# Two mixers of a macaron trunk: work order and delays laid out anew, a merge in six steps, an output norm that keeps the norm of q inside it

## The chip, the cores and the metric

The kernel runs on one core of a Trainium2 chip as one program. The metric is device time in microseconds (us) of one execution. Its engines are named as the profile names them: PE (TensorE matmuls; PEld are its weight loads), DVE (VectorE), ACT (ScalarE), POOL (GpSimd) and SP (SyncE, whose queue issues the transfers). Tensors live in SBUF; PE writes to PSUM, which has eight banks.

## The reference, cut to what matters

256 tokens of width 1024 go through two layers. Each layer is an FFN half step, a mixer and a second FFN half step, all with a norm before and a norm after. The mixer runs a gated DeltaNet (eight heads of 128) and a causal convolution module side by side:

```python
for i in range(DEPTH):
    f = swiglu_ffn(rmsnorm(x, ffn1_norm_pre[i]), ffn1_w_in[i], ffn1_w_out[i])
    x = x + 0.5 * rmsnorm(f, ffn1_norm_post[i])
    h = rmsnorm(x, mix_norm_pre[i])
    qkv, z, beta_logit, a_logit, glu_in, gates = jnp.split(h @ mix_w_in[i], SPLITS, axis=-1)
    y_a = gated_deltanet(qkv, z, beta_logit, a_logit, ...)   # short convolution, l2norm(q), l2norm(k),
                                                             # triangular solve, scan, rmsnorm(o) * silu(z), @ w_o
    y_b = conformer_conv(glu_in, ...)                        # glu, 31-tap convolution, layernorm, silu, @ w_o
    g_a, g_b = jnp.split(jax.nn.sigmoid(gates), 2, axis=-1)
    x = x + rmsnorm((g_a * y_a + g_b * y_b) @ mix_w_out[i], mix_norm_post[i])
    f = swiglu_ffn(rmsnorm(x, ffn2_norm_pre[i]), ffn2_w_in[i], ffn2_w_out[i])
    x = x + 0.5 * rmsnorm(f, ffn2_norm_post[i])
```

The output norm sees o, which is linear in q, and q was divided by its own norm: `o = rmsnorm(o, norm_w) * silu(z)`.

## The kernel before, in words

**Products.** Every large product is made in three matmuls of a split operand (high times high, high times low, low times high). A weight piece of 128 by 1024 comes in by DMA (raw), ACT rounds it (whi), and DVE or POOL makes the rest (wlo). Eight pieces stand in a ring.

**PE's order is written out.** PE runs in program order. The mixer (line 1128) works through the chunks of PLAN (line 38): glu (g0 to g3), keys (k1, ka, kb), values (v0, v1), queries (q0, q1), z0, z1 and the gates a0 to b1. The by-channel chunks (all g, k, v and q but the first two and ka) leave their products in two PSUM banks each, of four; a chunk two later takes the same banks. Then come three output products: the convolution's, the heads', and the common one (proj_out, line 908).

**Small work is slipped in by ticks.** Between the big matmuls of a chunk, after every three matmuls of 512 columns or six of 256, `Lanes.tick` (line 235) is called. When a chunk ends, the jobs that stand beside it in PLAN are added. A job is a generator; each of its steps issues instructions for several engines. DELAY (line 45) gives the ticks before its first step and between steps, AFTER the jobs that must be done before, LATE the ticks between their end and its start. BEFORE names jobs that are run to their end when a chunk's results are taken out (line 1576): vt0 and qt0 by z0 and a0, qt1 by z1 and a1, merge by b0 and b1. In front of the convolution's output product the job cn is run to its end, in front of the heads' product everything is.

**Fillers.** The taps of the long convolution (c0 to c3, conv31, line 1179; `cacc` in the profile) and the triangular solve on POOL (inv, line 1379) have no delays between steps. A tick issues them as long as the engine's estimated time is less than `ahead` (DVE) or `aheadp` (POOL) in front of PE's. The estimate adds up vector_us (line 95) or pool_us for each operation; DVE and POOL keep the program's order there (`in_order`).

**The jobs that the prediction speaks of.** f_... is the take-out of a chunk: for keys, values and queries the short convolution (conv4, line 1203; `c` in the profile), in steps start on ACT, taps on DVE, silu on ACT, for each of two pairs of heads. vt, qt and kt turn values, queries and keys to tokens and take their norms; qt also makes q times k (qk). sim makes the matrices of the triangular solve, inv solves their 32 by 32 diagonal blocks, and merge (line 1407) joins the blocks to 128 by 128 for both groups of four heads: turn the diagonal blocks, multiply below the diagonal (two steps for 64, two for 128), each time with ACT copies from PSUM back to the operands. In the kernel before, most of its steps hold one group or half of one. s0 and s1 (lines 1523, 1541) are the two parts of the scan; s1's first step ends in eight DVE corrections of vr that its second step's product reads. on0 and on (o_scale, line 1710) are the output norm of the two halves of the tokens: squares on ACT, a power on POOL, eight products on DVE. cn and cn1 are the layer norm of the convolution. pre0 and pre1 (line 693) bring the normed x into the next product's layout.

**Line numbers.** The profile's lines are those of helpers: L134 issues for DVE and POOL, L154 is any matmul, L160 a transpose on PE, L189 any ACT operation. Tiles tell the work apart: `mm` is a big product, `tr` a transpose, `gd` a small product.

Of the kernel before, what the change touches and what calls it, by code (L numbers as in the profile page):

```python
# [15 lines left out]
P = 128  # L16
# [30 lines left out]
    "ffn": (3, 2, 8, 12, 0), "pre0": (12, 12, 10, 0, 21, 2), "pre1": (14, 43, 4, 12, 8), "yt0": (10, 0, 10, 10, 26),  # L47
    "yt1": (10, 2, 0, 3, 3), "f_g0": (3, 0, 2, 9, 1), "f_g1": (5, 1, 1, 1), "c0": (0, 16, 0),
    "f_k1": (0, 1, 3, 1, 1, 3), "f_ka": (3, 0, 3), "decays": (12, 4, 2, 15, 4), "dts": (50, 3, 0, 0, 19, 19),
# [15 lines left out]
    "qs": ("qt0", "qt1"), "s0": ("merge", "vt0", "vt1", "qt0", "qt1"), "s1": ("s0",),  # L65
    "cn": ("c0", "c1", "c2", "c3", "s1"), "cn1": ("cn",), "on": ("s1", "on0"), "on0": ("s0", "qs"),
# [6 lines left out]
LATE = {"inv": 20, "cn": 12, "sim0": 5, "sim1": 6, "merge": 7, "dts": 14}  # L73

POOL = {*range(7, 10), *range(11, 14), 16, *range(18, 21), 22, 23, 25, *range(29, 33), 35, 36, 38, 39, *range(41, 45), *range(47, 50), 51, 53, 55, 58, 60, 61, 63, *range(65, 69), *range(70, 73), 77, 78, 85}
# [11 lines left out]
CFG = dict(stat=1000, conv=50, ev=300, tok=4, st=4, post=-800, pre=1000, fin=None, turn=100, tokens=-100, glu=100, dec=200, dts=500, kt=300, vt=0, qt=50, inv=1000, sim=100, merge=-400, scan=50, norm=-800, onorm=-100, yt=-400, w=50, forms=100, far=14, depth=9, land=1.8, slack=1.2, apart=3, beat=1.0, tails=4, ahead=1.5, lag=6, free=3, aheadp=3, lag2=3, bias=2, held=1)  # L87

KIND = {"f_g0": "glu", "f_g1": "glu", "f_g2": "glu", "f_g3": "glu", "decays": "dec", "dts": "dts", "kt0": "kt", "kt1": "kt",
        "vt0": "vt", "vt1": "vt", "qt0": "qt", "qt1": "qt", "qs": "qt", "inv": "inv", "sim0": "sim", "sim1": "sim",  # L90
# [4 lines left out]
def vector_us(name, size, k):  # L95
    return 0.1 + size / 960.0


def pool_us(name, size, k):
    if k.get("op") == ALU.pow:  # L100
        return 0.4 + 0.16 * size
    if name == "tensor_tensor":
        return 0.05 + 2.3e-3 * size if size > 600 else 0.19 + 1.7e-3 * size
    return 0.2 + (4e-3 if name == "tensor_scalar" else 1e-3) * size

# [222 lines left out]
class Stream:  # L328
# [83 lines left out]
    def plan(self, lanes):  # L412
        if lanes is not None:
            self.planned, self.lanes, lanes.stream, self.begun = True, lanes, self, self.pe.at
# [7 lines left out]
        else:  # L422
            for p in self.pieces[self.taken:self.nload]:
                self.force(p)
            self.planned, self.lanes.stream, self.lanes = False, None, None

# [60 lines left out]
    def issue(self, eng, t, p, kind):  # L487
# [4 lines left out]
        for c in p.parts if p.form else [slice(0, n)]:  # L492
            if kind == "sum":
                a, b = (r.part(c) for r in p.ins)
                with prio(self.tc, "w"):
                    eng.tensor_tensor(p.raw.part(c), a, b, op=ALU.subtract)
            elif kind == "high":
                self.to_high(p, c)
            else:
                self.to_low(p, c, eng)  # L500
        setattr(p, {"sum": "summed"}.get(kind, kind), eng.at)
# [38 lines left out]
def trunk(ctx: ExitStack, tc: tile.TileContext, x_in, wfirst, consts, feat, pch, tokp,  # L540
# [587 lines left out]
    def mixer(xt, l, after_mix):  # L1128
# [96 lines left out]
        rq = small(16, "rq", bufs=1)  # L1225
        rq2 = small(16, "rq2", bufs=1)
# [180 lines left out]
        def merge():  # L1407
            ps = [None, None]
            for gp in (1, 0):
                at = AT[gp]  # L1410
                for tb in range(2):
                    ts = slice(tb * 4, tb * 4 + 4)
                    pt = ps_gd()
                    for hl in range(4):
                        for b in (0, 64, 32):
                            bs = slice(b, b + 32)
                            T.matmul(pt[bs, hl, bs], U[gp][bs, tb * 4 + hl, bs], ident[bs, bs], start=True, stop=True)
                    for b in (0, 64, 32):
                        S.copy(at[b:b + 32, ts, b:b + 32], pt[b:b + 32, :, b:b + 32])
                    yield  # L1420
            for gp in (1, 0):
                at, ps[gp] = AT[gp], ps_gd([P, 16, 32])
                for th in range(8):
                    for b in (0, 64):
                        T.matmul(ps[gp][b + 32:b + 64, th, :], at[b:b + 32, th, b + 32:b + 64], at[b:b + 32, th, b:b + 32],
                                 start=True, stop=True)
                for b in (0, 64):
                    S.copy(at[b + 32:b + 64, :, b:b + 32], ps[gp][b + 32:b + 64, 0:8, :])
                W.memset(at[0:32, :, 32:64], 0.0)
                yield  # L1430
            for gp in (1, 0):
                at, u, p = AT[gp], U[gp], ps[gp]
                for th in range(8):
                    for b in (0, 64):
                        T.matmul(p[b:b + 32, 8 + th, :], at[b + 32:b + 64, th, b:b + 32], u[b + 32:b + 64, th, b + 32:b + 64],
                                 start=True, stop=True)
                    T.matmul(p[32:64, 8 + th, :], u[32:64, th, 32:64], at[32:64, th, 0:32], start=True, stop=True)
                for b in (0, 64):
                    S.activation(u[b:b + 32, :, b + 32:b + 64], p[b:b + 32, 8:16, :], AF.Copy, scale=-1.0)
                S.activation(at[32:64, :, 0:32], p[32:64, 8:16, :], AF.Copy, scale=-1.0)  # L1440
                yield

            def inner(gp, th):
                T.matmul(ps[gp][64:128, th, :], AT[gp][0:64, th, 64:128], AT[gp][0:64, th, 0:64], start=True, stop=True)

            def outer(gp, th):
                T.matmul(ps[gp][0:64, th, :], AT[gp][64:128, th, 0:64], U[gp][64:128, th, 64:128], start=True, stop=True)

            ps[1] = ps_gd([P, 8, 64])
            for th in range(8):  # L1450
                inner(1, th)
# [451 lines left out]
```

## Time and profile before

| | |
|---|---|
| median of 3 runs | 1338.12 us (1337.29 to 1340.12) |
| the profiled execution | 1336.74 us, its span 1335.0 us |
| PE, PEld, DVE, ACT, POOL busy | 98%, 83%, 77%, 58%, 28% |
| granted TensorE clock | 0.999 |
| PE's longest waits in total, span | ACT cf 3.4, ACT vT 2.9, ACT qT 2.8 us |
| chain that ended last | PE 66%, DVE 19%, DMA 6%, ACT 5% |

In a row of a timeline stand start, duration, engine, line, operation, result and operands, form and count; in brackets the idle time of the engine before it and what ended that. In a row of the windows stand the stretch and its length, then for PE, PEld, DVE, ACT and POOL the busy time and the number of instructions, the granted clock, the share of the DMA engines and GB/s. In a group of instructions stand its count, its busy time in total, the mean of one in ns, and the idle time before it. In a row of the waits stand who waited for whom, the sum, the number and the longest. A matmul's shown duration is longer than the distance to the next one, since they are pipelined; that distance is what it costs PE. The first mixer lies at about 176 to 482 us, the second at 837 to 1143 us; between and around them are the FFNs.

### The profile page before, as it was taken

The page shows a single profiled execution, that of the slowest core. Times are in us where ns is not written, and L with a number is a line of the kernel's source. Part 1 is how long each engine was busy: PE and PEld are TensorE (multiplying, and loading weights), DVE is VectorE, ACT ScalarE, POOL GpSimd, SP SyncE. Part 2 cuts the span into 40 slices and gives each one's busy share as a digit, 9 for nine tenths or more (in the row PEclk, how much of TensorE's full clock was granted, in tenths as well). Part 3 has the DMA queues.
Part 4 walks back from the last instruction along what each step waited for, and adds up shares of the span by engine and source line. Part 5 has one row for each costly group of instructions (what it writes and reads, how often), then busy time and mean ns, then how long its engine had stood idle before and what let it go on. Part 6 is the DMA issues. An engine that isn't in the chain of part 4 may idle for free.

```text
span 1335.0 us, 20602 instructions
## 1 busy us (share of the span) xinstructions
PE 1310.3 (98%) x7371; PEld 1112.0 (83%) x7371; DVE 1032.8 (77%) x1816; ACT 771.1 (58%) x1259; POOL 369.1 (28%) x332
## 2 busy tenths in 40 slices
PE   9999999999999999999999999999999999999998
PEld 6888879997787888888888888899977878888886
DVE  6889655999975776897577985579999666678973
ACT  7556547675656545565455564577656564555651
POOL 0000017798853200000000000277997431000000
PEclk9999999999999999999999999999999999999999
DMA  8885846562643766857668767464546437487481
GB/s 292 298 282 154 299 158 206 175 210 98 196 154 126 241 222 220 267 175 265 200 226 269 239 199 259 147 235 174 167 133 198 152 134 252 171 275 247 146 286 60
DMA packets 115014, 273.78 MB, mean 205 GB/s; under 512 B 24128, under 2 KB 47712, under 8 KB 114912
## 3 DMA queue, kind: packets, MB, share of 16 engines
q1 hardware_dynamic: 114624, 272.40, 61.2%
q8 instruction: 58, 0.95, 0.3%
q14 instruction: 44, 0.36, 0.1%
q10 hardware_dynamic: 288, 0.07, 0.0%
HBM read 256.68 MB, written 15.75 MB: 204 GB/s over the span
## 4 chain that ended last, share of the span: by engine, by line
PE 66%; DVE 19%; DMA 6%; ACT 5%; issue 3%; POOL 1%; SPq 0%; DVEq 0%; POOLq 0%; ACTq 0%
PE mm L154 61%; DVE wlo L134 6%; DVE cacc L134 4%; PE gd L154 3%; DMA raw<-w2i 2%; DVE c L134 2%; DMA raw<-mw 2%; ACT whi L189 2%; PE tr L160 2%; DVE sum L134 1%; DVE ag L134 1%; DMA x<-x 1%; DVE at L134 1%; DMA raw<-w1i 1%; ACT dt L189 1%
## 5 line engine op out<-in xcount | busy, mean ns | idle before, releaser
L154 PE MATMUL mm<-whi,xt 128*128 128x512 f32 (+1 forms) x1888 | 598.8, 391 | 3.4 <-ACT qT L189 2.2
L189 ACT CAST whi<-raw 128x1024 fp32r<-128x1024 f32 (+1 forms) x424 | 434.6, 1035 | 282.5 <-PE mm L154 63.3
L134 DVE TENSOR_TENSOR wlo<-raw,whi 128x1024 fp32r<-128x1024 f32 (+1 forms) x316 | 375.7, 1211 | 108.8 <-ACT whi L189 106.3
L154 PEld LDWEIGHTS mm<-whi,xt 128*128 128x128 f32 x1888 | 352.8, 188 | 76.7 <-ACT qT L189 3.0
L154 PE MATMUL mm<-wlo,xt 128*128 128x512 f32 (+1 forms) x944 | 364.9, 387 | 0.0
L134 POOL TENSOR_TENSOR wlo<-raw,whi 128x1024 fp32r<-128x1024 f32 (+1 forms) x108 | 253.7, 2366 | 144.7 <-ACT whi L189 142.3
L154 PE MATMUL mm<-whi,act 128*128 128x512 f32 x704 | 218.3, 390 | 0.0
L154 PEld LDWEIGHTS mm<-wlo,xt 128*128 128x128 f32 x944 | 177.7, 188 | 33.1
L134 POOL TENSOR_TENSOR rpost<-ss,exp 128x1 f32<-128x1 f32 x12 | 6.5, 538 | 660.6 <-DVE ss L134 660.6
L134 DVE SCALAR_TENSOR_TENSOR cacc<-hT,pc,cacc 128x254 f32<-128x254 f32 (+28 forms) x464 | 179.3, 463 | 0.2
L154 PE MATMUL mm<-xt,whi 128*128 128x256 f32 x960 | 175.5, 285 | 0.8 <-ACT qT L189 0.6
L154 PEld LDWEIGHTS mm<-whi,act 128*128 128x128 f32 x704 | 132.2, 188 | 27.5
L154 PEld LDWEIGHTS mm<-xt,whi 128*128 128x128 f32 x960 | 149.3, 192 | 1.9 <-ACT qT L189 0.9
L154 PE MATMUL mm<-wlo,act 128*128 128x512 f32 x352 | 137.3, 390 | 1.0 <-DVE wlo L134 1.0
L154 PE MATMUL mm<-xt,wlo 128*128 128x256 f32 x480 | 135.8, 283 | 0.0
L154 PEld LDWEIGHTS mm<-xt,wlo 128*128 128x128 f32 x480 | 91.9, 192 | 0.0
L154 PEld LDWEIGHTS mm<-wlo,act 128*128 128x128 f32 x352 | 66.1, 188 | 15.6 <-DVE wlo L134 2.2
L189 ACT ACTIVATE ag<-mm,rstd 128x256 f32<-128x256 f32 x76 | 33.8, 471 | 31.6 <-PE mm L154 31.5
L189 ACT ACTIVATE jk<-mm 128x512 f32<-128x512 f32 x24 | 14.3, 597 | 64.5 <-PE mm L154 64.5
L134 DVE TENSOR_TENSOR act<-way,act 128x512 fp32r<-128x512 f32 x44 | 30.2, 686 | 21.9 <-ACT act L189 21.9
L134 DVE SCALAR_TENSOR_TENSOR c<-mm,pc,c 128x255 f32<-128x255 f32 (+2 forms) x108 | 43.6, 472 | 2.4 <-ACT c L189 2.4
L134 DVE SCALAR_TENSOR_TENSOR ag<-mm,rstd,ag 128x256 f32<-128x256 f32 x76 | 33.9, 477 | 13.5 <-ACT ag L189 13.5
(215 smaller groups left out, 1458.5 us busy)
## 6 DMA issues: line engine op xcount, KB each, us to landing
raw<-mw SPq DMA_DIRECT2D x168, 512.0 KB, 3.6
raw<-w2i SPq DMA_DIRECT2D x80, 512.0 KB, 5.1
raw<-w1i SPq DMA_DIRECT2D x76, 512.0 KB, 4.9
raw<-w1o SPq DMA_DIRECT2D x44, 512.0 KB, 4.8
raw<-w2o SPq DMA_DIRECT2D x44, 512.0 KB, 4.8
way<-way SPq DMA_DIRECT2D x112, 64.0 KB, 2.1
way<-way SPq DMA_DIRECT2D x28, 256.0 KB, 3.7
wbc<-feat SPq DMA_DIRECT2D x13, 512.0 KB, 4.8
```

Source lines behind the costliest of these rows:

```text
L134: r = op(out, *a, **k)
L154: r = self.eng.matmul(o, w, x, **k)
L160: r = self.eng.transpose(*a)
L189: r = op(out, *a, **k)
```

## The change

The order of the chunks stays but for v1, which comes before g2. Jobs stand beside other chunks: kt1 with k1, kt0 last in kb's list, c3, vt1 and both qt with q0, c2 and s1 with q1, cn1 with z1, on0 with a0. Nearly all delays of the mixer's jobs are new, as are LATE and the set POOL (which weight pieces outside the planned stretch get their low half on POOL). The operation estimate for DVE is larger for all but the smallest operations; the FFNs' plan keeps the old one. The merge runs both groups in one step, one stage apart. The job qs is gone: o is no longer divided by q's norm. Instead q's sum of squares, scaled by RMS_EPS, is added to the mean square of o in the place of the constant RMS_EPS, which gives the same result.

```diff
 PLAN = [
...
+    ("g0", ["f"]),
+    ("k1", ["f", "sim1", "kt1"]),
+    ("ka", ["f", "decays", "dts"]),
+    ("g1", ["f", "c0"]),
+    ("kb", ["f", "sim0", "inv", "c1", "kt0"]),
+    ("g3", ["f"]),
+    ("v1", ["f"]),
+    ("g2", ["f"]),
+    ("q0", ["f", "qt1", "qt0", "c3", "vt1"]),
+    ("q1", ["f", "cn", "s1", "c2"]),
+    ("v0", ["f", "vt0"]),
+    ("z0", ["s0"]),
+    ("z1", ["merge", "cn1"]),
+    ("a0", ["on0"]),
+    ("b0", []),
+    ("b1", []),
+    ("a1", ["on"]),
 ]
```

The delays that the prediction uses:

```diff
-"pre1": (14, 43, 4, 12, 8),            "f_q1": (1, 1, 3, 1, 0, 0, 2),        "f_v0": (1, 0, 1, 1, 0, 0, 0)
+"pre1": (13, 44, 6, 32, 6),            "f_q1": (0, 0, 0, 4, 2, 0, 16),       "f_v0": (0, 0, 1, 4, 0, 25, 10)
-"merge": (4, 3, 2, 2, 2, 3, 2, 2),     "s1": (11, 5, 3, 6, 1, 1),            "cn": (52, 20, 4, 30, 3, 0, 41, 8)
+"merge": (4, 4, 2, 15, 5, 13, 9, 4),   "s1": (18, 0, 0, 15, 0, 10),          "cn": (49, 24, 0, 36, 14, 6, 2, 4)
-"c2": (6, 0, 0, 0), "c3": (19, 20, 24, 44), "dts": (50, 3, 0, 0, 19, 19),    "inv": (76, 4, 9, 0, 14, 16, 9, 1)
+"c2": (20, 20, 10, 6), "c3": (23, 1, 17, 7), "dts": (0, 3, 0, 0, 29, 0),     "inv": (76, 3, 19, 5, 13, 0, 0, 0)
-LATE = {"inv": 20, "cn": 12, "sim0": 5, "sim1": 6, "merge": 7, "dts": 14}
+LATE = {"inv": 18, "cn": 5, "sim0": 7, "sim1": 0, "merge": 8, "dts": 13, "qt0": 0, "s1": 0, "s0": 4, "qt1": 6, "vt0": 2, "vt1": 17, "kt0": 0, "kt1": 2}
-CFG = dict(..., ahead=1.5, ..., aheadp=3, ..., bias=2, ...)
+CFG = dict(..., ahead=1.2, ..., aheadp=2.5, ..., bias=1.5, ...)
 def vector_us(name, size, k):
-    return 0.1 + size / 960.0
+    return (0.126 if size > 40 else 0.07) + size / 960.0
```

The merge's stages are generators of single products, named turned, first, second, third and fourth; each has its ACT copies (turned_out and so on). Turned, first and second use 32-row blocks, third and fourth 64-row blocks. This loop runs them:

```diff
+            stages = [(turned, turned_out), (first, first_out), (second, second_out), (third, third_out), (fourth, fourth_out)]
+            for i in range(len(stages) + 1):
+                if i:
+                    yield
+                at = [(stages[k], gp) for k, gp in ((i, 1), (i - 1, 0)) if 0 <= k < len(stages)]
+                sums = [list(stage[0](gp)) for stage, gp in at]
+                n = 8
+                for th in range(n):
+                    for s in sums:
+                        for go in s[th * len(s) // n:(th + 1) * len(s) // n]:
+                            go()
+                for stage, gp in at:
+                    stage[1](gp)
```

The output norm:

```diff
-            V.tensor_scalar(vq[:, gp * 8:gp * 8 + 8], ss, float(P), P * 1e-6, op0=ALU.mult, op1=ALU.add)
+            V.tensor_scalar(vq[:, gp * 8:gp * 8 + 8], ss, P * RMS_EPS, P * 1e-6 * RMS_EPS, op0=ALU.mult, op1=ALU.add)
...
-        def q_scale():
-            yield from ()
-            power(rq, vq, -0.5)
-            W.tensor_tensor(rq2, rq, rq, op=ALU.mult)
...
-            W.tensor_tensor(ve, rq2t, sso, op=ALU.mult)
-            W.tensor_scalar(v8, v8, 1.0 / P, RMS_EPS, op0=ALU.mult, op1=ALU.add)
+            V.scalar_tensor_tensor(ve, sso, 1.0 / P, vqt, op0=ALU.mult, op1=ALU.add)
             power(r8, v8, -0.5)
-            W.tensor_tensor(ro, ro, rqt, op=ALU.mult)
```

More of the change, by code (lines that the diff above doesn't have):

```diff
@@ L64 @@
     "qt0": ("f_q0", "vt0"), "qt1": ("f_q1", "vt1"),
-    "qs": ("qt0", "qt1"), "s0": ("merge", "vt0", "vt1", "qt0", "qt1"), "s1": ("s0",),
-    "cn": ("c0", "c1", "c2", "c3", "s1"), "cn1": ("cn",), "on": ("s1", "on0"), "on0": ("s0", "qs"),
+    "s0": ("merge", "vt0", "vt1", "qt0", "qt1"), "s1": ("s0",),
+    "cn": ("c0", "c1", "c2", "c3", "s1"), "cn1": ("cn",), "on": ("s1", "on0"), "on0": ("s0", "qt0", "qt1"),
 }
@@ L85 @@
 USERS = {"12": (("t1", "summed"),), "22": (("22", "low"), ("t2", "summed")), "11": (("t3", "low"),), "21": (("21", "low"), ("t4", "summed"))}
-CFG = dict(stat=1000, conv=50, ev=300, tok=4, st=4, post=-800, pre=1000, fin=None, turn=100, tokens=-100, glu=100, dec=200, dts=500, kt=300, vt=0, qt=50, inv=1000, sim=100, merge=-400, scan=50, norm=-800, onorm=-100, yt=-400, w=50, forms=100, far=14, depth=9, land=1.8, slack=1.2, apart=3, beat=1.0, tails=4, ahead=1.5, lag=6, free=3, aheadp=3, lag2=3, bias=2, held=1)
+CFG = dict(stat=1000, conv=50, ev=300, tok=4, st=4, post=-800, pre=1000, fin=None, turn=100, tokens=-100, glu=100, dec=200, dts=500, kt=300, vt=0, qt=50, inv=1000, sim=100, merge=-400, scan=50, norm=-800, onorm=-100, yt=-400, w=50, forms=100, far=14, depth=9, land=1.8, slack=1.2, apart=3, beat=1.0, tails=4, ahead=1.2, lag=6, free=3, aheadp=2.5, lag2=3, bias=1.5, held=1)
 KIND = {"f_g0": "glu", "f_g1": "glu", "f_g2": "glu", "f_g3": "glu", "decays": "dec", "dts": "dts", "kt0": "kt", "kt1": "kt",
-        "vt0": "vt", "vt1": "vt", "qt0": "qt", "qt1": "qt", "qs": "qt", "inv": "inv", "sim0": "sim", "sim1": "sim",
+        "vt0": "vt", "vt1": "vt", "qt0": "qt", "qt1": "qt", "inv": "inv", "sim0": "sim", "sim1": "sim",
         "merge": "merge", "s0": "scan", "s1": "scan", "cn": "norm", "cn1": "norm", "on": "onorm", "on0": "onorm",
@@ L104, in pool_us, with plain_us @@
     return 0.2 + (4e-3 if name == "tensor_scalar" else 1e-3) * size
+def plain_us(name, size, k):
+    return 0.1 + size / 960.00
 class Clocked:
@@ L1441, in merge @@
[L1441 to L1451, printed above, removed]
-            S.copy(AT[1][64:128, :, 0:64], ps[1][64:128])
-            yield
@@ L1454, in merge @@
[L1454 to L1464 removed]
+                        yield lambda th=th, b=b: T.matmul(p[b:b + 32, th, :], at[b + 32:b + 64, th, b:b + 32],
+                                                          u[b + 32:b + 64, th, b + 32:b + 64], start=True, stop=True)
@@ new lines, in second, with second_out, third @@
+                    yield lambda th=th: T.matmul(p[32:64, th, :], u[32:64, th, 32:64], at[32:64, th, 0:32], start=True, stop=True)
+            def second_out(gp):
+                at, u, p = AT[gp], U[gp], ps[gp]
+                for b in (0, 64):
+                    S.activation(u[b:b + 32, :, b + 32:b + 64], p[b:b + 32, 0:8, :], AF.Copy, scale=-1.0)
+                S.activation(at[32:64, :, 0:32], p[32:64, 0:8, :], AF.Copy, scale=-1.0)
+            def third(gp):
+                at = AT[gp]
+                pb[gp] = ps_gd([P, 8, 64])
+                for th in range(8):
+                    yield lambda th=th: T.matmul(pb[gp][64:128, th, :], at[0:64, th, 64:128], at[0:64, th, 0:64], start=True, stop=True)
@@ new lines, in third_out, with fourth, fourth_out @@
+            def third_out(gp):
+                S.copy(AT[gp][64:128, :, 0:64], pb[gp][64:128])
+            def fourth(gp):
+                at, u = AT[gp], U[gp]
+                for th in range(8):
+                    yield lambda th=th: T.matmul(pb[gp][0:64, th, :], at[64:128, th, 0:64], u[64:128, th, 64:128], start=True, stop=True)
+            def fourth_out(gp):
+                S.activation(U[gp][0:64, :, 64:128], pb[gp][0:64], AF.Copy, scale=-1.0)
+            stages = [(turned, turned_out), (first, first_out), (second, second_out), (third, third_out), (fourth, fourth_out)]
```

72 lines of the change are left out of this document (28 added, 44 removed), and 20 rows, old and new, of tables (DELAY, PLAN).

## Prediction

> **What bounds the kernel now.** I read the page's busy table first, then the two mixers by windows against an FFN, then who made PE wait, then the timelines of PE and DVE around the longest waits.
>
> ```profile
> PE 1310.3 (98%) x7371; PEld 1112.0 (83%) x7371; DVE 1032.8 (77%) x1816; ACT 771.1 (58%) x1259; POOL 369.1 (28%) x332
> 176.00:482.00 306.00, 298.83 (x2110) 263.18 (x2109) 245.30 (x534) 187.30 (x353) 180.58 (x157) 1.00 0.53 174
> 837.00:1143.00 306.00, 299.20 (x2112) 263.33 (x2111) 245.81 (x534) 186.94 (x351) 180.77 (x157) 1.00 0.52 174
> 500.00:840.00 340.00, 339.35 (x1507) 280.67 (x1506) 259.32 (x352) 188.69 (x258) 3.24 (x6) 1.00 0.69 228
> ```
>
> TensorE (PE) is busy nearly always. The FFN stretch 500 to 840 us has 0.65 us without PE work; each mixer stretch of 306 us has about 7 us. The granted clock is 1.00 in all three. So a schedule of the mixers can win at most some 7 us a layer by removing waits, and beyond that only by making PE's own work shorter. The waits of the first mixer, and the two most frequent of them in their place:
>
> ```profile
> PE tr L160 <- ACT cf L189: 1.7, 1, 1.7
> PE tr L160 <- ACT vT L189: 1.5, 1, 1.5
> PE mm L154 <- ACT qT L189: 1.4, 2, 1.1
> PE tr L160 <- ACT stg L189: 0.9, 1, 0.9
> PE gd L154 <- ACT sq L189: 0.5, 1, 0.5
> 302.42 0.28 PE L154 MATMUL mm<-xt,wlo 128*128 128x256 f32 x1
> 302.99 0.36 PE L154 MATMUL mm<-xt,whi 128*128 128x256 f32 x1 [0.29 <-ACT qT L189]
> 310.45 2.42 DVE L134 SCALAR_TENSOR_TENSOR c<-mm,pc,c 128x255 f32<-128x255 f32 x6
> 313.93 2.43 DVE L134 SCALAR_TENSOR_TENSOR c<-mm,pc,c 128x255 f32<-128x255 f32 x6
> 300.00:345.00 45.00, 41.70 (x257) 36.40 (x256) 44.79 (x101) 25.72 (x51) 38.54 (x61) 1.00 0.40 122
> L134 DVE SCALAR_TENSOR_TENSOR cacc<-hT,pc,cacc 128x254 f32<-128x254 f32 (+28 forms) x464 | 179.3, 463 | 0.2
> ```
>
> ACT is named for qT and vT, but it only finishes what DVE delivers: the taps of the short convolution (c<-mm). From 300 to 345 us DVE is busy 44.79 of 45. PE ends q1 at 302.6; the planner lays q1's first taps 2 ticks behind (f_q1: 1, 1), a tick being the matmuls between two calls of the planner, 6 of 0.12 us here. So they belong at about 304, and ran at 310.45: DVE is 6 us behind its plan. The reason is in the last row. A tap costs 179.3/464 = 0.386 us; the planner's vector_us gives 0.1 + 240/960 = 0.350 at the mean width of 240. It fills DVE with taps of the long convolution (FILL) up to `ahead` by that estimate, so every tap leaves 0.036 us of debt: some 160 operations between 255 and 316 make 5.8 us, which is the lag seen.
>
> **The change, part by part.** The profiled execution took 1336.74 us (span 1335.0 and 1.7 around it), 1.4 below the median of the three runs, 1338.12; the sum of differences is applied to both.
>
> *New estimate, fillers ordered anew.* vector_us becomes 0.126 + 240/960 = 0.376, within 0.010 of the tap's 0.386; `ahead` goes from 1.5 to 1.2 us. c3 and c2 move behind q0 and q1 with 23 and 20 ticks of delay, so the short taps of q1 and v0 meet a DVE with no debt of 6 us. I take the waits for qT and vT as gone: 1.4 + 1.5 = 2.9 us here. The second mixer runs the same program with the same windows to 0.4 us, so 5.8 together. Restarting costs more than the shown idle time: from 302.42 to 302.99 are 0.57 us for a matmul of 0.12 and a wait of 0.29, so 0.16 each; six waits, 1.0 us. Together **-6.8**, bounds 0 (the lag stays) and -6.8. What is late next is the long convolution: its taps move 4 to 6 us later, into 381 to 388 us, where DVE has this pause, and its readers come with cn at 408:
>
> ```profile
> 388.80 0.35 DVE L134 SCALAR_TENSOR_TENSOR vr<-gd,neg_eg,vr 128x128 f32<-128x128 f32 x1 [7.42 <-PE gd L154]
> 389.84 1.90 DVE L134 SCALAR_TENSOR_TENSOR vr<-gd,neg_eg,vr 128x128 f32<-128x128 f32 x7
> 387.70 1.95 PE L154 MATMUL gd<-state,kT 128*128 128x128 f32 x16
> 392.90 1.95 PE L154 MATMUL gd<-vr,u 128*128 128x128 f32 x16
> ```
>
> *Merge.* The same 160 small products a layer, in 6 steps of both groups in place of 11. What a step costs PE is the time between the big matmuls on its two sides, less their usual 0.23 us:
>
> ```profile
> 352.57 0.39 PE L154 MATMUL mm<-whi,xt 128*128 128x512 f32 x1
> 352.89 0.45 PE L154 MATMUL gd<-cst,u 32*32 32x32 f32 x24
> 353.26 0.50 PE L154 MATMUL mm<-whi,xt 128*128 128x512 f32 x1
> 358.45 0.39 PE L154 MATMUL mm<-whi,xt 128*128 128x512 f32 x1
> 358.77 0.69 PE L154 MATMUL gd<-at 32*32 32x32 f32 x32
> 359.39 0.50 PE L154 MATMUL mm<-whi,xt 128*128 128x512 f32 x1
> 370.62 0.40 PE L154 MATMUL mm<-whi,xt 128*128 128x512 f32 x1
> 370.95 0.27 PE L154 MATMUL gd<-at 64*64 64x64 f32 x1
> 371.06 0.22 PE L154 MATMUL gd<-at 64*64 64x64 f32 x1
> 371.12 0.22 PE L154 MATMUL gd<-at 64*64 64x64 f32 x1
> 372.03 0.50 PE L154 MATMUL mm<-whi,xt 128*128 128x512 f32 x1
> 373.29 0.40 PE L154 MATMUL mm<-whi,xt 128*128 128x512 f32 x1
> 374.69 0.50 PE L154 MATMUL mm<-whi,xt 128*128 128x512 f32 x1
> ```
>
> A turning step (four blocks deep) costs 0.46, a 32-row step (eight deep) 0.71, a 64-row step 1.17. The step at 370.62 holds two kinds of product, and costs 1.18: products on other blocks of the array ride along free. Before: 4 x 0.46 + 4 x 0.71 + 3 x 1.17 = 8.2 us. After: turning of one whole group, eight deep, 0.71; two steps of two 32-row kinds, 0.71 if they overlap and 1.2 if not (0.5 of depth added): I take 0.85, nearer the overlap that 370.62 shows; a step that alternates a 64-row with three 32-row products eight times: 1.17 if free, 1.67 if in turn, plus 16 changes of size; then 1.18 and 1.17. No row shows a change between 32 and 64. The nearest: going into 64 rows, the second record comes 0.11 after the first, the next 0.06, so 0.05 of entry; a turning step costs 0.46 for 0.26 of depth, so 0.1 for each of its two changes. I take 0.05: 1.67 + 0.8 = 2.47. After: 0.71 + 2 x 0.85 + 2.47 + 1.18 + 1.17 = 7.2, a gain of 1.0 a layer, **-2.0**; bounds 5.65 (free throughout, -5.1) and 8.5 (in turn throughout, 0.1 a change, +0.6).
>
> *New waits inside merge and scan.* The third merge step now comes 2 ticks (1.4 us) behind the second, and needs four of its ACT copies; two steps of one group used to be apart. Four copies of 0.36 to 0.38 and a hand-over of 0.2 make 1.7: a wait of 0.3 to 0.4, and 1.05 more where a weight cast stands before them.
>
> ```profile
> L189 ACT COPY at<-gd 32x256 f32<-32x256 f32 x4 | 1.5, 364 | 0.7 <-PE gd L154 0.6
> L189 ACT CAST whi<-raw 128x1024 fp32r<-128x1024 f32 x8 | 8.4, 1048 | 3.5 <-DMA raw<-mw 3.4
> ```
>
> I take 0.5, bounds 0 and 1.5: **+1.0**. In s1 the second step moves from 5 ticks behind the first to 1. PE's first step ended at 389.4 (16 records of 0.11 from 387.70), so the second is due at 390.1, and the corrections it reads ended at 391.74. Its second half reads the last of them 0.9 into it, so PE waits about 0.7, or nothing if the two hT products between them (0.8 us) go elsewhere. I take 0.5: **+1.0**. Behind this wait stand all of PE's big matmuls.
>
> *Entry.* pre1 turns x at tick 13, not 14. The tick lost is three matmuls, 0.68 us, and the data already was the last to arrive:
>
> ```profile
> 197.21 0.39 PE L154 MATMUL mm<-whi,xt 128*128 128x512 f32 x1
> 197.80 0.41 PE L160 MATMUL tr<-cst,xw 128*128 128x128 f32 x2 [0.20 <-DVE xw L134]
> ```
>
> So PE waits 0.88 here, and likewise in the second layer: **+1.4**, bounds 0 and +1.4.
>
> *Output norm.* Out go, a layer, POOL's two operations on rq (2.90 and 0.22) and three of the five in each o_scale; in come two small DVE operations.
>
> ```profile
> L134 POOL TENSOR_TENSOR rq<-vq,exp 128x16 f32<-128x16 f32 x1 | 2.9, 2902 | 0.1
> 394.10 8.51 DVE L134 SCALAR_TENSOR_TENSOR o<-o,ro,z 128x128 f32<-128x128 f32 x8
> 433.88 0.60 PE L160 MATMUL tr<-cst,o 128*128 128x128 f32 x4
> ```
>
> The first half's products end at 402.6 and PE reads them at 433.88; 31 us of cover, so **0**. Without the cover each removed microsecond would be one of PE.
>
> *Left as they were.* BEFORE still forces vt0 and qt0 out at z0's end and qt1 at z1's, and cn is still forced out in front of the convolution's output product (24 ticks between its steps, 20 before): the waits for cf and stg stay. inv still starts 76 ticks behind kb and dts about 50 behind ka, so SP's transfers of dA, dU and the gate rows, and POOL's solve behind them, keep their places: 0. The FFNs keep their plan (plain_us is the old vector_us): 0.
>
> Sum: -6.8 - 2.0 + 1.0 + 1.0 + 1.4 = **-5.4**. The profiled execution becomes 1331.3, the median **1332.7 us**.
>
> **Rivals.** *Changes of size drain PE.* The Trainium skill, "TensorEngine Tiling (Array Packing)", Tiling Modes, says that changing the tiling mode drains the TensorE. The 0.05 and 0.1 above may be just that; for changes between 32 and 64 rows the trace neither bears it out nor refutes it. From the rows: 16 changes at the 0.1 of the turning step make the mixed step 3.3 instead of 2.47, 0.8 a layer, so 1334.3; with the two doubled steps in turn as well, 1335.7. Chance 0.17.
>
> *DVE stays behind.* The debt may come less from the estimate than from the load: DVE has 44.79 of 45 us of work whatever its order. Then the 6.8 stay, the merge's 2.0 and the new 3.4 nearly cancel, and the time is 1338 to 1339.5, which is no change. For it: nothing is removed from DVE. Against: the pause of 7.42 us at 381 and the agreement of debt and lag. Chance 0.17.
>
> *The output norm gets in front of the scan.* This one is slower. on0 and s1 now both come free in the tick that ends s0. If DVE's queue gets the eight o products ahead of the eight corrections, the corrections start when the products end instead of at 388.80, and PE, due with the second step of s1 at 390.1, waits for all of it. With the products at 0.27 each they end at 394.1 + 2.2 = 396.3, the corrections 2.4 later: a wait of some 8 us a layer, and with products as slow as the 8.51 row some 14. So 1348 to 1360. It decides as soon as one product stands before the corrections. Against it: the corrections are ready some 5 us earlier, and scan has the higher priority (50 to -100). Chance 0.08.
>
> *All terms at their better end:* -6.8 - 5.1 and no new waits, 1326.2. Chance 0.12.
>
> **How the numbers follow.** The forecast, 1332.7 with 1330 to 1335 of its own, has 0.46. A measurement of this kernel tells 0.2% (2.7 us) from no change. Faster than 1335.4: the forecast, the better end and most of the drains (0.13), **0.71**; within: DVE behind with the rest, **0.17**; slower: the norm in front, and DVE behind with all new waits at their upper bound, **0.12**. The range takes in the better end with the wait for sq gone too (0.5 a layer), and on the other side DVE behind with some of the new waits: **1325 to 1340**.
>
> **What would show it.** Right: no wait for qT and vT between 285 and 330 us of the new profile, q1's taps within 3 us of PE's end of q1; six clusters of small products of together 7 us; short new waits at gd<-u,at and gd<-vr,u, and 0.9 at tr<-xw. Wrong: DVE's taps as late as before; alternating 32 and 64 rows at over 3 us; a wait of several microseconds at gd<-vr,u with o<-o,ro,z before it; or a new wait in a place that none of these names, such as PE on a weight's low half.

## The result, and the profile after

After the change the median is 1342.05 us, against 1338.33 us of the kernel before on the same chips: ratio 1.0026, 95% interval 1.0017 to 1.0035. The forecast was 1332.7 us; the kernel became slower by some 3.5 us. One of the 16 executions after the change took 3859.61 us and is left out of the ratio. The profiled execution took 1340.24 us (span 1338.1, 3.1 longer than before).

The windows of after, the two mixers and an FFN (columns as before):

```profile
PE 1312.7 (98%) x7371; PEld 1114.0 (83%) x7371; DVE 1037.5 (78%) x1828; ACT 769.2 (57%) x1247; POOL 344.4 (26%) x308
176.00:484.00 308.00, 300.97 (x2116) 264.94 (x2115) 249.64 (x541) 186.95 (x346) 168.05 (x145) 1.00 0.53 175
837.00:1146.00 309.00, 301.31 (x2112) 265.18 (x2111) 246.14 (x539) 185.90 (x347) 168.53 (x145) 0.99 0.52 172
500.00:840.00 340.00, 339.28 (x1505) 280.22 (x1504) 258.62 (x351) 187.50 (x257) 3.25 (x6) 1.00 0.69 228
```

The FFN is nearly what it was. Each mixer still has 7 to 7.7 us without PE work. The windows of after are 2 and 3 us longer than those of before; between the same products PE's own work grew by 0.9 us in the first mixer and by 2.1 in the second. Of these 2.1, 1.7 are one stretch of 3.41 us from 1017.7 us on, in which the granted clock was 0.5. The longest waits of the first mixer, after:

```profile
PE tr L177 <- ACT cf L206: 1.7, 1, 1.7
PE mm L171 <- DVE hT L151: 1.4, 1, 1.4
PE mm L171 <- DVE wlo L151: 0.8, 1, 0.8
PE tr L177 <- ACT stg L206: 0.5, 1, 0.5
PE gd L171 <- DVE vr L151: 0.5, 1, 0.5
PE gd L171 <- ACT at L206: 0.4, 1, 0.4
```

The waits for qT and vT (2.9 us) are gone, as forecast; cf stays, as forecast; hT and the weight halves (wlo) are new. Where the time went shows best when the same big product is compared in both kernels (each issues 6007 of `mm`; the n-th of one against the n-th of the other, start times from the traces):

| at (us of before) | what lies behind it | after, us later | e10 below, us later |
|---|---|---|---|
| 284 | first chunks | -1.04 | -0.17 |
| 300 | first half of q1 | +0.25 | -0.51 |
| 349 | q1, v0, z0: qT and vT | -3.67 | -4.06 |
| 434 | merge, scan, convolution | -3.16 | -5.06 |
| 475 | output products | +0.23 | -3.99 |
| 837 | common product, FFNs | +0.88 | -3.05 |
| end | second mixer, last FFN | +3.15 | -8.09 |

So the change earned 3.9 us a layer between 300 and 349, and lost it at three places: 1.3 at the start of q1, what merge should have brought, and 3.4 under the output products. The second mixer repeats this to 0.2 us, but for the stretch from 349 to 434, where it loses 2.1 instead of 0.5 us: there lies the half clock.

**The wait in q1.** PE in after (start, duration, operation, and in brackets the wait), and the product on DVE that it waits for:

```profile
289.51 0.28 PE L171 MATMUL mm<-xt,wlo 128*128 128x256 f32 x1
...
291.18 0.50 PE L171 MATMUL mm<-xt,whi 128*128 128x256 f32 x2 [1.39 <-DVE hT L151]
290.65 0.47 DVE L151 SCALAR_TENSOR_TENSOR hT<-mm,pc,sg 128x256 f32<-128x256 f32 x1
```

q1 takes the PSUM banks of g2, the chunk two before it. The change gives the second half of g2's take-out 12 ticks more (f_g2 from 0, 1, 0, 1 to 2, 0, 12, 1), and moves g2 behind v1, so the product hT that empties the bank is issued too late.

**The mixed merge step.** The first and last rows of the fourth step, which alternates eight times:

```profile
363.62 0.39 PE L171 MATMUL mm<-whi,xt 128*128 128x512 f32 x1
363.94 0.33 PE L171 MATMUL gd<-at 64*64 64x64 f32 x2
364.20 0.22 PE L171 MATMUL gd<-u,at 32*32 32x32 f32 x2
...
364.26 0.19 PE L171 MATMUL gd<-at,u 32*32 32x32 f32 x1
364.38 0.32 PE L171 MATMUL gd<-at 64*64 64x64 f32 x2
...
367.48 0.50 PE L171 MATMUL mm<-whi,xt 128*128 128x512 f32 x1
```

From 363.62 to 367.48 are 3.86 us, less the usual 0.23: 3.63, where 2.47 was forecast. Each jump between the sizes (364.26 to 364.38) shows some 0.12 us. The other steps cost 0.72, 0.91, 1.15, 1.17 and 1.17 without their waits: 8.75 in all, against 8.3 of the old eleven steps. The 1.15 hold some 0.2 of restarting behind a wait: where the third step didn't wait (e15 below), it cost 0.90.

**The weight halves under the output products.** DVE and POOL in after, then the chain from POOL's second low half to a wait of PE:

```profile
457.88 2.19 DVE L151 TENSOR_TENSOR wlo<-raw,whi 128x1024 fp32r<-128x1024 f32 x1 [1.39 <-ACT whi L206]
456.59 2.41 POOL L151 TENSOR_TENSOR wlo<-raw,whi 128x1024 fp32r<-128x1024 f32 x1 [10.65 <-ACT whi L206]
459.33 3.01 POOL L151 TENSOR_TENSOR wlo<-raw,whi 128x1024 fp32r<-128x1024 f32 x1 [0.33 <-ACT whi L206]
462.36 0.33 SPq L380 DMA_DIRECT2D raw<-mw  x1
467.97 1.05 ACT L206 CAST whi<-raw 128x1024 fp32r<-128x1024 f32 x1 [2.04 <-DMA raw<-mw]
469.05 1.22 DVE L151 TENSOR_TENSOR wlo<-raw,whi 128x1024 fp32r<-128x1024 f32 x1 [1.86 <-ACT whi L206]
470.33 0.50 PE L171 MATMUL mm<-wlo,yt 128*128 128x512 f32 x1 [0.76 <-DVE wlo L151]
```

The new set POOL gives GpSimd five low halves between 430 and 475 us, the old one three. One that DVE makes alone takes 1.23; the one that starts at 457.88, while POOL's runs, ends 1.1 us after POOL's ends, and POOL's next takes 3.01 instead of 2.4. The Trainium skill, "SBUF — State Buffer", Who interferes with whom, describes this as one exclusively locked port pair; the rows agree. POOL's second low half ends at 462.34 us, and only then, at 462.36, SP issues the next load of raw, of which there are four buffers. The cast, the low half and PE's product of this piece follow one another without a pause from its landing on. In before the same load is issued 0.3 us later, at 462.64, but there PE comes to this stretch some 3 us later than in after, and doesn't wait.

### The profile page after: what moved, and what is told of

Read it like the earlier page. It is cut to its first block, busy times and chain, and to the rows that moved or that the text cites. A ratio compares the mean times of both kernels' runs of the same rounds, so it can differ in the third digit from the quotient of the medians.

```text
span 1338.1 us, 20588 instructions
## 1 busy us (share of the span) xinstructions
PE 1312.7 (98%) x7371; PEld 1114.0 (83%) x7371; DVE 1037.5 (78%) x1828; ACT 769.2 (57%) x1247; POOL 344.4 (26%) x308
## 4 chain that ended last, share of the span: by engine, by line
PE 64%; DVE 17%; DMA 7%; ACT 5%; issue 4%; POOL 3%; SPq 0%; DVEq 0%; POOLq 0%; ACTq 0%
PE mm L171 60%; DVE cacc L151 6%; DVE wlo L151 4%; DMA raw<-mw 3%; DMA raw<-w1i 3%; ACT whi L206 3%; PE gd L171 2%; POOL wlo L151 2%; DVE c L151 1%; PE tr L177 1%; DMA raw<-w2i 1%; ACT dt L206 1%; DVE sum L151 1%; POOL rk L151 1%; DVE qT L151 1%
## 5 line engine op out<-in xcount | busy, mean ns | idle before, releaser
L151 DVE TENSOR_TENSOR wlo<-raw,whi 128x1024 fp32r<-128x1024 f32 (+2 forms) x324 | 389.5, 1221 | 133.6 <-ACT whi L206 131.8
L151 POOL TENSOR_TENSOR wlo<-raw,whi 128x1024 fp32r<-128x1024 f32 (+1 forms) x100 | 235.8, 2375 | 150.8 <-ACT whi L206 143.5
```

Source lines behind the costliest of these rows:

```text
L151: r = op(out, *a, **k)
```

## The experiments

All ratios are to the kernel before on the same chip, with 95% intervals; 0.001 is 1.34 us. The theory at the start was that the change's own parts (merge, waits) behave as traced, and that the loss comes from parts that the forecast set at nothing. The rivals were that the new merge lowers the clock or is worse than the old one, and that it is all noise of the clock.

**e1, the kernel before against itself.** No edit.

> The kernel before, unchanged, for the granted clock of its own runs. The runs of the changed kernel show a mean clock between 0.994 and 0.999, and its profile has half clock from 1017.7 to 1021.2 us, inside the second mixer's merge. Theory A, the new merge brings the clock down: here the clock is 0.999 in every run and the times keep within 3 us around 1338. Theory B, such drops fall on any kernel by chance: clocks of 0.995 to 0.998 here as well, about as often, and the difference of 3.7 us is all schedule.

Ratio 1.0009 (0.9997 to 1.0020): what two runs of one kernel may differ by. Its profile also has a half-clock stretch (331.2 us), so these aren't a trait of the new merge.

**e2, the step not alternated.**

```diff
-                n = 8
+                n = 1 if i == 3 else 8
```

> The changed kernel, but the merge step that alternates 64-row and 32-row products makes all eight 64-row products first and then the twenty-four 32-row ones: 3 changes of size in place of 17. If the changes of size are what the step costs (3.63 us measured): 1.17 + 0.5 + one more change of about 0.1 = 1.8, so 1.8 less a layer and 1338.4 in all; under theory A also fewer clock drops, to 1337. If alternating is not the price, the step stays near 3.6 and the time at 1342.

Ratio 1.0018 (1.0006 to 1.0031). The step falls from 3.63 to 1.79 us, as expected, but the median gained only about 1 us: its profile has a wait of 2.8 us for vr and two half-clock stretches (392.1, 1020.1). e13 comes back to this.

**e3, the old merge in the new plan** (the eleven steps and their delays put back).

> The changed kernel with the merge of before (11 steps, its delays 4, 3, 2, 2, 2, 3, 2, 2) and all else as changed. The merge cost PE 8.34 us a layer before and 8.75 after, with new waits of 0.45 in the first and 1.57 in the second mixer. Theory M, the merge is the cause: 0.9 and 2.0 less, and no half clock (1.7): 1337.5 with a clock of 0.999. Rival P, the cause are the waits for low halves at the end of the mixer: then 0.8 to 1 less only, 1341.

Ratio 1.0079 (1.0063 to 1.0095), with new waits for vr (2.6) and vn (1.5) in the first mixer. So in the new plan a return to the eleven steps and their delays costs some 7 us more; the merge as a whole is not what made after slow, though one of its steps may still be too dear.

**e4, the old set POOL in after; e5, the new set POOL in before** (the same edit the other way round).

```diff
-POOL = {8, 9, 10, 13, 16, 19, 23, 25, 31, ...}
+POOL = {*range(7, 10), *range(11, 14), 16, *range(18, 21), 22, ...}
```

> The changed kernel with the set POOL of before, which decides which weight pieces outside the planned stretch get their low half on POOL. The changed kernel has five new waits of PE between 443 and 470 us (0.3 + 0.5 + 0.4 + 1.0 of extra distance, 2.3 in all) and likewise in the second mixer. Rival P: they come from pieces 75, 81 and 83 on POOL; they go, 4.5 less, 1337.5. Theory M (merge and clock): those waits move elsewhere, 1341 to 1342.

> Before with one thing of the change alone: its set POOL, the numbers of the weight pieces whose low halves GpSimd makes. Theory P: the set by itself makes weight halves late at the end of each mixer, since VectorE's own low halves stretch from 1.15 to 2.2 us beside GpSimd's. Then before becomes about 3.2 us slower (1341.5 us, ratio 1.0024), with PE waits for wlo and whi of about 2 us between 440 and 472 us. Rival S: the set hurts only where VectorE's fillers were moved too. Then the time is that of before (ratio 0.999 to 1.001) and there are no such waits.

e4: 1.0002 (0.9992 to 1.0012), 3.2 us less than after. e5: 1.0036 (1.0022 to 1.0049), 4.8 us more than before. Waits of e5 in its first mixer:

```profile
PE mm L154 <- POOL wlo L134: 1.8, 1, 1.8
PE tr L160 <- ACT cf L189: 1.7, 1, 1.7
PE tr L160 <- ACT stg L189: 1.7, 1, 1.7
```

The wait for POOL's low half is new, that for stg has grown from 0.9. So the set by itself costs 3 to 5 us, in either plan; theory P holds and its rival S falls.

**e6, after with the old f_g2; e7, the same with the old set POOL and the step not alternated.**

```diff
-"f_g2": (2, 0, 12, 1)
+"f_g2": (0, 1, 0, 1)
```

> After with the waiting times of f_g2 of before (0, 1, 0, 1 in place of 2, 0, 12, 1), so that the product that empties g2's second bank is issued 12 ticks earlier. Theory G: the wait of 1.4 us (1.55 with the restart) at the first matmul of q1 goes, and nothing takes its place: 2 x 1.55 = 3.1 us, so 1339.0 us (ratio to before 1.0003). Rival: VectorE is full there, and what goes in front delays qT or vT by as much: waits for them of 0.5 us or more come back and the time stays at 1341 to 1342.5 us.

> After with three things at once: the set POOL of before, the fourth merge step with all 64-row products ahead of the 32-row ones, and the waiting times of f_g2 of before. If the three prices add up as measured so far (set POOL 3.2 us off by its own run, f_g2 3.1 by the trace, the step 1.1 by its run and 3.7 by the trace), 1342.1 - 3.2 - 3.1 - (1.1 to 3.7) = 1332.1 to 1334.7 us, which beats both kernels (ratio 0.9955 to 0.997). Rival: what is taken off PE comes back as waits for VectorE (vr, xw) within the same mixer, and the time is 1337 to 1339 us.

e6: 1.0045 (1.0030 to 1.0060), slower than after; e7: 0.9993 (0.9983 to 1.0002). In both the wait for hT went, but more than that was lost in merge, where PE waits 3.6 and 3.8 us for at in the first mixer. GpSimd's solve and PE's merge, in e7 and then in after:

```profile
299.18 0.87 POOL L151 MEMSET iu<- 128x512 f32 x3
338.68 0.23 POOL L151 TENSOR_TENSOR iu<-iu 128x16 f32<-128x16 f32 x1
350.84 1.05 ACT L206 CAST whi<-raw 128x1024 fp32r<-128x1024 f32 x1 [3.14 <-DMA raw<-mw]
354.19 0.25 PE L171 MATMUL gd<-at 32*32 32x32 f32 x4 [3.34 <-ACT at L206]
```

```profile
293.64 0.86 POOL L151 MEMSET iu<- 128x512 f32 x3
332.72 0.24 POOL L151 TENSOR_TENSOR iu<-iu 128x16 f32<-128x16 f32 x1
```

The solve takes 39 us in both. In e7 it starts and ends 6 us later, while PE comes to merge at the same time. So f_g2's 12 ticks were not only a loss: with them the solve starts early. (In e6 the low halves in front of the solve on POOL wait for ACT's casts; why these are late stays open.)

**e8, the new estimate alone in before** (vector_us, ahead, aheadp, bias).

> Before with the estimate of VectorE's times alone: vector_us, plain_us, ahead 1.2, aheadp 2.5 and bias 1.5, with the old order, waiting times, merge, set POOL and output norm. Theory D (the forecast's first term): the lag of 6 us in q1's taps is a debt of the estimate, so it vanishes: the taps come within 3 us of the end of q1 and the waits for qT and vT go, up to 6.8 us, so 1331.5 to 1334 us. Rival O: the debt is not in the estimate but in the order (c3 and c2 due beside q0 and q1), so the waits for qT and vT stay at 2 us or more a layer and the time is 1337 to 1339.5 us.

Ratio 1.0380 (1.0363 to 1.0398), which neither theory gives. Its first mixer, POOL and SP, then ACT and PE:

```profile
304.82 0.87 POOL L138 MEMSET iu<- 128x512 f32 x3
295.73 16.94 SPq L367 DMA_DIRECT2D raw<-mw  x7
339.17 1.31 SPq L1407 DMA_DIRECT2D dU<-iu  x2
344.56 1.04 ACT L193 CAST whi<-raw 128x1024 fp32r<-128x1024 f32 x1 [24.68 <-DMA raw<-mw]
347.01 0.78 PE L164 MATMUL tr<-cst,vT 128*128 128x128 f32 x2 [17.28 <-ACT vT L193]
```

The solve starts 8 us later than in before (297.00); its result's transfer, dU<-iu, stands ahead of raw in SP's queue and waits for its end, so no weights land, ACT stands for 24.68 us at a cast with vT's silu behind it, and PE with it. Yet part of theory D holds: the waits for qT (1.4 us a layer in before) are gone in both mixers, and q1's first taps start at 312.24, 4.7 us behind q1's end at 307.53, where before has 7.8 (310.45 and 302.70). So the estimate shortens the lag, but it doesn't work in the old order; the new order without it was not run.

**e9, e7 with the solve's ten transfers on GpSimd's queue.**

```diff
-                nc.sync.dma_start(dv[par], ur[par * 64:par * 64 + 64])
+                nc.gpsimd.dma_start(dv[par], ur[par * 64:par * 64 + 64])
...
-                    nc.sync.dma_start(U[gp][js, :, js], du[gp, :, j].rearrange("t s c -> s t c"))
+                    nc.gpsimd.dma_start(U[gp][js, :, js], du[gp, :, j].rearrange("t s c -> s t c"))
```

> The three parts undone (set POOL, fourth step, f_g2) as in the run before, and the ten transfers that bring the solved blocks from iu through dU to u issued from GpSimd's queue in place of SyncE's. Theory Q: in that run the second merge step waited 3.34 us for ACT's copies, ACT stood behind a weight cast, the cast behind a transfer of raw, and that one on SyncE behind dU<-iu, which waits for GpSimd's solve until 338.9 us. With the queue free, raw is loaded between 323 and 339 us, the wait of 3.34 goes in both layers, and so does the half clock that followed it: 3.3 x 2 plus up to 1.7 x 2, so 1328 to 1332 us (ratio 0.992 to 0.995). Rival R: merge itself needs u, which comes when the solve ends; issue on GpSimd costs it some us more, so u lands later than 345 us, the first merge step waits for it, and the time is 1337 to 1343 us.

Ratio 1.0073 (1.0059 to 1.0088); theory Q falls. POOL and SP in e9:

```profile
330.46 2.40 POOL L151 TENSOR_TENSOR wlo<-raw,whi 128x1024 fp32r<-128x1024 f32 x1
...
339.96 3.49 POOL L1423 DMA_DIRECT2D u<-dU  x6 [0.22 <-issue]
332.89 21.48 SPq L380 DMA_DIRECT2D raw<-mw  x8
```

SP has nothing before it but raw, and still the loads start at 332.89, when the low half that POOL begins at 330.46, among the last operations of the solve, has ended: there are four buffers of raw, and POOL's low halves hold them. Here it is POOL's order that keeps the weights back, not SP's queue. The issues (6 of them 3.49 us) then delay POOL's next low halves, and the waits for at come to 4.3 us.

**e10, f_g2 at 2, 0, 9, 1**, with the old set POOL, the step not alternated, and pre1 back at 14, 43.

> After with the set POOL of before, the fourth step not alternated, f_g2 at 2, 0, 9, 1 (three ticks less) and pre1 at 14, 43 as in before. Theory G: three ticks are 2 us, more than the wait of 1.4 us for hT at the first matmul of q1; it goes, while the 9 ticks left keep the convolution's products behind those of sim, so that the solve still ends by 333 us and merge isn't held up; xw's wait goes back to 0.2. From 1339.2 (set POOL alone): -3.1 (hT), -1.1 to -3.7 (step), -1.4 (xw), so 1331 to 1334 us (ratio 0.994 to 0.9965). Rival: the solve moves to 336 us or later as with f_g2 of before, the wait for ACT's at in merge is 3 us again, and the time is 1337 to 1340 us.

Ratio 0.9929 (0.9917 to 0.9941), 1328.61 us: 9.5 us less than before, 4 less than the forecast for the change, and 2.4 below what was expected of this run. Its longest waits in the first mixer, and the end of its solve:

```profile
PE tr L177 <- ACT cf L206: 1.7, 1, 1.7
PE gd L171 <- ACT at L206: 1.5, 3, 0.9
PE mm L171 <- DVE ss L151: 0.5, 1, 0.5
334.31 0.23 POOL L151 TENSOR_TENSOR iu<-iu 128x16 f32<-128x16 f32 x1
```

hT is gone without a late solve. From the start of the solve's last operation to the big product before the first merge step are 13.0 us in after (345.72), 11.0 in e10 (345.34) and 7.5 in e7 (346.16), and PE then waits 0.4, 1.5 and 3.8 us for at. In the second mixers it is 1.0, 1.5 and 3.3 us at 13.0, 11.0 and 7.9. So the later the solve ends before merge, the longer merge waits; but up to 1.0 us of this wait is there at 13 us too, where ACT's casts stand in front of the copies, so the traces don't give a distance from which on the solve costs nothing.

**e11, the new merge alone in before; e12, the new output norm alone in before.**

> Before with the merge of after alone (six steps of both groups, with its waiting times 4, 4, 2, 15, 5, 13, 9, 4). The forecast's term was -1.0 a layer. By the trace of after the products cost PE 8.75 us a layer against 8.34, so +0.4 a layer and 1339.0 us, if nothing else moves. Rival: the longer waiting times between the steps (39 ticks against 27) bring the scan later and against the end of z0, where it is forced out: +2 us or more a layer, 1342 us and above, with new waits for vr or vn.

> Before with the output norm of after alone (no q_scale: GpSimd's power of 2.9 us and its product go, two of three operations on GpSimd in each o_scale become one of VectorE). The forecast's term was 0, since 31 us lie between the norm's products and their reader: 1338.0 to 1339.5 us, ratio 0.999 to 1.001. Rival: GpSimd free 4 us earlier a layer makes other low halves there, and the time differs by over 0.15% to either side.

e11: 1.0108 (1.0089 to 1.0127), the rival: 2.2 us of waits for at and new ones for xhat (1.0) and ct (0.7), probably because the new delays between the steps don't fit the old order; no run separates the steps from their delays. e12: 0.9998 (0.9989 to 1.0007): nothing, as forecast.

**e13 to e16: one part of e10 put back at a time, and one step more.** e13 has f_g2 and pre1 of the change, e14 the alternated step, e16 the new set POOL; e15 is e10 with the third merge step two ticks later (merge 4, 4, 4, 13, ...).

> After with the set POOL of before and the fourth merge step not alternated; f_g2 and pre1 as in after. Theory H: the alternated step costs twice, 1.84 us itself (3.63 against 1.79) and, where most of it falls into one stretch of 3.41 us of the clock's grid, half clock for the next 3.41 us (370.0 us in the run with the set POOL alone). So against that run's 1339.2 us: -3.7 and up to -2 of clock, 1333.5 to 1335.5 us, mean clock .998 or above. Rival: the changes of size are hidden behind waits for VectorE as in the first run without them, which moved the median by 1.1 us only: 1337.5 to 1339 us.

> The fastest kernel so far (1328.6 us: set POOL of before, step not alternated, f_g2 2, 0, 9, 1, pre1 14, 43) with the fourth merge step alternated again. Theory H: +3.7 us for 2 x 1.84, and half-clock stretches of 3.41 us at this step in some runs, so 1332.5 to 1336 us, a wider spread of the times and a mean clock under .9985. Rival (changes of size cost little once nothing else is late): 1329 to 1331 us.

> The fastest kernel so far with the third merge step 4 ticks behind the second in place of 2 (merge 4, 4, 4, 13, 5, 13, 9, 4). In its profile PE waits 1.30 us at this step for ACT's copies. Theory S (the solve on GpSimd with ACT's casts behind it sets this point, so a later step loses nothing): the wait goes, up to 2 x 1.3 = 2.6 us, so 1326 to 1327.5 us. Rival: the copies behind the step come later by as much and the wait moves to the fourth step or to vr, so 1328 to 1330 us.

> The fastest kernel so far with the set POOL of the change put back. Theory P: the set costs the same 3 us in this schedule as in before (3.6 to 4.8 by its run) and in after (2.9 by its run), through waits for weight halves at the end of each mixer: 1331.5 to 1333.5 us, with waits for wlo, whi of 1.5 us or more between 435 and 475 us. Rival: the set was made for the order of the change, and only f_g2 and the step were wrong: 1327.5 to 1329.5 us.

| kernel | set POOL | step | f_g2, pre1 | ratio (interval) | mean clock |
|---|---|---|---|---|---|
| after | new | alternated | new | 1.0026 (1.0017 to 1.0035) | .9968 |
| e2 | new | not | new | 1.0018 (1.0006 to 1.0031) | .9974 |
| e4 | old | alternated | new | 1.0002 (0.9992 to 1.0012) | .9966 |
| e13 | old | not | new | 0.9967 (0.9954 to 0.9979) | .9984 |
| e14 | old | alternated | 9 ticks, old | 0.9975 (0.9963 to 0.9987) | .9964 |
| e16 | new | not | 9 ticks, old | 0.9964 (0.9952 to 0.9977) | .9986 |
| e10 | old | not | 9 ticks, old | 0.9929 (0.9917 to 0.9941) | .9986 |
| e15 | old | not | 9 ticks, old | 0.9916 (0.9900 to 0.9931) | .9990 |

Each part, from pairs of rows that differ in it alone: set POOL 3.2, 4.7 and 6.8 us; the alternated step 1.1, 4.7 and 6.2; f_g2 with pre1 3.6, 5.1 and 7.2. Each difference is uncertain by some 2 us, but every pair has the same sign. Theory P holds, and so does H but in e2: its edit gains 1.1 us beside the new set POOL, where PE then waits for vr, and 4.7 beside the old one (e4 to e13). So the prices don't simply add. f_g2 and pre1 were put back together; by the traces f_g2 is worth 2.8 to 3.1 (hT) and pre1 1.4 (xw, 0.9 and 0.2 us). A third value of f_g2 can be compared alone: e7 is e13 with 0, 1, 0, 1, is 3.5 us slower, and its solve ends at 338.68 instead of 333.71. e15 isn't told from e10: its wait at the third step falls from 1.30 to 0, but one of 1.65 appears at the second.

**The clock.** The step's own 1.84 us make 3.7 of the 4.7 and 6.2; the rest fits the mean clock in the last column, lower by 0.0018 and 0.0022 with the step alternated. Which stretch loses its clock differs: in e14's profile both half-clock stretches follow PE's wait at the third merge step, while in e4 one follows the alternated step itself (last section). So that the alternation lowers the clock is shown by the means, and only in part by the traces. e14's stretch with the second and third merge steps and the next (the granted clock is the third number from the end):

```profile
352.57:355.98 3.41, 2.12 (x85) 1.49 (x84) 3.41 (x11) 3.28 (x8) 3.38 (x5) 1.00 0.73 243
355.98:359.39 3.41, 3.41 (x10) 2.64 (x9) 3.30 (x9) 2.37 (x5) 2.97 (x2) 0.50 0.65 174
```

In the second PE finishes 10 big products where it would do 15: 1.7 us lost.

**e17, e10 with the step in four rounds** (`n = 4 if i == 3 else 8`).

> The fastest kernel but one (e10) with the fourth merge step in four rounds of 64-row and 32-row products instead of one (eight in the change). Theory H prices each change of size: the step has 15 changes inside at eight rounds and costs 3.63, 1 at one round and 1.79, so 0.131 each; at four rounds there are 7, and the step is to cost 1.79 + 6 x 0.131 = 2.58 us, the whole 1328.6 + 1.6 = 1330.2 us, with the clock at .998 or above. Rival: the cost is not that of the change but of every small product that stands behind another size (a weight load that can't go ahead), then the halved number of blocks changes little: 3.2 us or more in the step, 1332 us or more.

```profile
365.18 0.39 PE L171 MATMUL mm<-whi,xt 128*128 128x512 f32 x1
365.50 0.44 PE L171 MATMUL gd<-at 64*64 64x64 f32 x4
...
367.99 0.50 PE L171 MATMUL mm<-whi,xt 128*128 128x512 f32 x1
```

The step costs 2.58 us (365.18 to 367.99, less 0.23), to the hundredth what 0.131 us for each change of size gives; the rival's 3.2 falls. The kernel as a whole has 0.9954 (0.9940 to 0.9968), 3.3 us over e10 where 1.6 were expected; its profile has a wait of 1.8 at the second merge step and half clock behind it, and its mean clock is .9978, below the .998 expected.

## Why the prediction was wrong, point by point

- **New estimate, fillers ordered anew (-6.8).** The waits for qT and vT went, and q1's first taps start at 305.92 us, 3.0 behind q1's end at 302.96, where before has 7.8: the outcome and the size were right (3.9 us a layer by the aligned products). The reason, a debt of the estimate, is half shown: e8 has the estimate alone, its taps come earlier and its waits for qT go, but it is 51 us slower, so the order is needed as well. What failed is what stands beside this term: the same new delays hold g2's banks for 12 more ticks, and PE waits 1.39 for hT in q1, for which the forecast has no term.
- **Merge (-2.0).** Failed by size: "I take 0.05" for a change between 32 and 64 rows, where the runs show 0.131 (3.63, 2.58 and 1.79 us at 15, 7 and 1 changes). The rival of the drains was right in kind, a price for each change (whether it is a drain no run shows), and even its 3.3 was too low. The two doubled 32-row steps cost 0.91 and 1.15 where 0.85 was taken. The upper bound is added up wrongly: 0.71 + 2 x 1.2 + 3.27 + 1.18 + 1.17 are 8.7, not 8.5, and the 8.75 measured lie at it. Not alternated, merge costs 6.91 without waits, below the 7.2 forecast. Beside it stood a term that the forecast didn't have: half clock in such a stretch (e4).
- **"Left as they were".** This is the step that failed outright. The set POOL is named in the change but has no term in the sum; it costs 3 to 5 us, through the place that the last sentence of the prediction named as a sign of its being wrong: PE on a weight's low half.
- **New waits in merge and scan (+2.0).** s1's second step waits 0.49 in the first mixer and not in the second; merge's third step waits 0.45 and 1.57 (1.05 of the latter put down to at). Right in size and in cause: in the first mixer no cast stands before the five copies that the step needs (they start at 350.77), in the second one of 1.05 us does (1011.34). GpSimd's solve, which makes this wait longer in e6 and e7, has no part in it here: in after it lies as far before merge as in before (13.0 and 13.1 us).
- **Entry (+1.4).** The wait for xw stays at 0.2 and 0.3 in after; with the old set POOL (e4, e13) it is the 0.9 forecast. Not a term of after.
- **Output norm (0), cf and stg staying.** Right (e12).
- **Rivals.** DVE did not stay behind, and the output norm did not get in front of the scan. The slower side was reached by no mechanism that was named for it.

The sum by the runs: -7.8 for qT and vT, +0.8 for merge's products, +2.0 and +0.5 for waits in merge and s1, +2.8 to 3.1 for hT, +3.2 for the set POOL, and 1 to 2 for the clock (mean .9968, before .9981): +2.5 to +3.8, where +3.5 was measured. The prices of waits are from one profile, those of the set POOL and the clock from runs, so this is a balance, not a proof of each term.

## What to carry to other kernels

A plan with many free numbers must be read number by number: a set or a delay that looks like bookkeeping (which engine makes a weight half, when a PSUM bank is emptied) can cost as much as the wait that the change removes, and each is a term of the sum. Before counting a removed wait as won, look for the slow engine off the path whose result comes next: here GpSimd, 26% busy, has a solve of 39 us, and merge waited the longer the later it ended (e6, e7). Keep products of one tile size together on TensorE; price each change of size, and look at what share of the array the stretch uses.

## What the runs showed of the hardware

**Half clock after half a window.** In the 19 profiles every change of the granted clock inside the kernel lies a whole number of 3.413 us stretches after the first. Of some 7,200 such stretches at full clock, the first and last few of each profile left out, 25 were followed by half clock. If each product counts from its start to the next one's, times its share of the array's rows, PE worked less than 0.495 of the stretch in 24 of these 25, and in only 4 of all the others. The 1.7 us wait for cf leaves 0.496 to 0.497 when it falls into one stretch, as here in before, and the clock stays:

```profile
1075.20:1078.60 3.40, 1.68 (x15) 1.39 (x13) 3.17 (x7) 3.25 (x9) 0.95 (x2) 1.00 0.45 154
```

PE need not be idle: in e4 the alternated step fills a stretch wholly, by rows to 0.42, and half clock follows:

```profile
366.60:370.00 3.40, 3.40 (x59) 2.52 (x58) 3.33 (x10) 0.00 (x0) 0.44 (x1) 1.00 0.69 234
370.00:373.40 3.40, 3.40 (x15) 2.67 (x14) 3.40 (x10) 3.14 (x6) 1.53 (x1) 0.50 0.02 5
```

So a wait over some 1.7 us can cost as much again, depending on where it falls, which differs from one execution to the next; the spread of the times agrees (e10 1328.1 to 1329.3 us in 5 executions, after 1339.2 to 1345.6 in 15). The Trainium skill, "TensorE: Matmul & The Clock Gate", What's actually happening, gives the stretch as 3413 ns, free-running, which agrees; it lets the clock fall after an idle stretch, and here a half idle one is enough. The weighting by rows fits these records; no run tests it alone.

**32-row products on different blocks** overlap. In after's first merge step 48 records on three blocks, which write one bank, start 11 ns apart on average (0.51 us); in the second 80 records, which write two banks, start 9 ns apart (0.70 us). So the step with 80 records costs 0.91 us and the one with 48 costs 0.72.
